# A hybrid conv/attention encoder step: one more projection block by seven products, two plain gates fewer, gate outputs in pairs of pieces, and another form and order of the loads between attention and the output products

## The chip, the cores and the metric

One core of a Trainium2 chip runs the whole program. The metric is device microseconds of one execution. The kernel before takes 1477.87 us (median of 3 runs, 1476.27 to 1478.02). All times are from those runs, from one profiled execution, or from its trace.

## What is computed

One inference step of a one-layer encoder: 1024 new prompt frames and 64 frames of a running stream, 1024 channels each, all in fp32. Cut to what matters:

```python
def mixer(xn, conv_prefix, attn_fn, w_in, w_conv, w_conv_out, w_attn_out, w_out):
    proj = xn @ w_in                                  # 1024 -> 5120
    cb, cc, ch, q, k, v, ga, gb = jnp.split(proj, ...)
    cv, conv_state = causal_conv(cc * ch, conv_prefix, w_conv)
    ya = (cb * cv) @ w_conv_out                       # 512 -> 1024
    o, new_k, new_v = attn_fn(heads(q), heads(k), heads(v))
    yb = o.reshape(B, L, ATT_DIM) @ w_attn_out        # 512 -> 1024
    merged = jax.nn.sigmoid(ga) * ya + jax.nn.sigmoid(gb) * yb
    return merged @ w_out, conv_state, new_k, new_v
# trunk: x += mixer(rmsnorm(x)); x += swiglu(rmsnorm(x)); rmsnorm(x)
# outputs too: the last 512 key and value rows; for the running stream its
# cache, rolled by 64 rows (448 old rows are copied, 64 new ones appended)
```

The gate projections `ga` and `gb` are 1024 channels wide: eight blocks of 128 rows each, over all T = 1088 frames.

## The kernel before

**Numbers.** Every fp32 operand is split into a high part (rounded to fp32r, the format the matmul takes) and a low part, what is left. A product is three matmuls: weights high by data high, weights high by data low, weights low by data high. `split(hi, lo, src)` does it with a copy on ACT and a subtraction on DVE (L126 to L130).

**Two ways to multiply.** A `Unit` (L202, `run` L246) computes two blocks of 128 output channels for all frames by a seven-product scheme of 2x2 blocks: 7 products x 4 slices of the contraction x 3 matmuls x 2 pieces of 272 frames = 168 matmuls of 128x272. Its inner loop gives each weight to two pieces `j` in turn, into two banks of one PSUM tile. A plain block goes through `product` (L323): for one piece of 272 frames, 24 matmuls in a row where the contraction is 1024 long, 12 where it is 512. Two plain blocks of 1024 take 2 x 4 pieces x 24 = 192 matmuls.

**Stages.** (1) normalisation, transposes, V. (2) twelve units: q, k, cc, ch, cb and two of the four pairs of blocks of `gb` (blocks 0 to 3), with the convolution on the side. The convolution's result times `cb` is u; `cb_done` (L699) splits it and stores both parts to DRAM in `u_d`. (3) the twelve plain gates of `GATES` (L335): eight blocks `a` and blocks 4 to 7 of `b`. `gate` (L805) copies each piece of 272 frames from PSUM (tag `mm`, 3 banks) to a buffer `gst` of `st_pool` (5 buffers) on ACT and stores it to DRAM through the POOL queue. Attention runs in between: `between()` (L1003) is called after a piece and lets `PER` = 2.7 of attention's 75 steps be emitted. (4) with `LAST` = 3 gates to go, what is left of attention is emitted, its buffers are given up, and u, the attention output ob, its reciprocal sums rc, and the first gates ga and gb are loaded on SP's queue (L1049 to L1066). ob times rc is split on chip. (5) the output products ya (from u) and yb (from ob), for m = 0 to 7, four pieces each, multiplied by the sigmoid of the gates out of PSUM (L1075 to L1100). (6) `w_out`, the second norm, twenty-two units of the up projections, the down projection, the final norm. In the ups, two copies from DRAM to DRAM (L1539) fill the old rows of the two cache outputs.

**Order.** The kernel is written in Tile: the program says which buffers and operations there are, and a scheduler that works before the run sets the order on each engine. Engines and queues then issue strictly in that order and wait on semaphores. In the names, `g` is a gate's PSUM bank (`g_2` is the piece that starts at frame 544), `gst` its buffer in SBUF, `wp` a plain weight (high), `low` the area of low parts, `xn` the normalised input, `pv`, `t`, `s` attention's PSUM tiles, `rc` the reciprocal sums.

The layouts matter to the change: `Acts` (L56) finds a slice of u or ob at `[:, l, k, o]` with rows of 1088 frames; the operands of the units keep two halves of 544 frames with padding between the parts (`operand`, L136).

```python
def product(out, w, x, o, n):
    kt = 4 * len(w)
    for k in range(kt):
        ...
        mm(out, a, first, start=k == 0, stop=False)
        mm(out, a, then, start=False, stop=False)
        mm(out, b, p, start=False, stop=k == kt - 1)
```

## Time and profile before

| What | Value |
|---|---|
| profiled execution | 1475.81 us |
| its span (first to last instruction) | 1473.8 us |
| median of the runs | 1477.87 us |
| PE busy | 1458.0 us, 10200 matmuls |
| DVE / ACT / POOL busy | 979.2 / 678.1 / 133.1 us |
| DMA | 264.72 MB, mean 180 GB/s |
| twelve units and what is between them | 68.3 to 323.1 us |
| gates with attention | 323.1 to 575.0 us |
| output products ya, yb | 575.0 to 671.1 us |

The page lists the busy time of each engine and the groups of instructions. Matmuls are pipelined: a record of a 272-column matmul is about 0.29 us long, but the next starts 0.12 to 0.13 us after it, so the pace has to be read from the starts of matmuls, not from their lengths, and a wait shorter than some 0.16 us leaves no idle time in the PE row.

### The profile page before, as it was taken

To read this page: it belongs to the slowest core of one execution; us is meant where nothing else is said; L and a number is where in the kernel's file an instruction comes from. 1 tells how busy PE (TensorE), PEld (TensorE's weight loads), DVE (VectorE), ACT (ScalarE), POOL (GpSimd) and SP (SyncE) were. 2 spreads that over 40 slices of the span, in tenths; PEclk is the share of its full clock that TensorE was granted. 3 is DMA by queue.
4 is the path that set the end of the run, shared out by engine and by line. 5 is a ranking of instruction groups with operands and counts; after the bars stand their busy time and mean duration, and the time that the engine had idled before them with its cause. 6 is when DMAs were issued, how large, how long until landed. Compare 5 with 4: busy or idle time off the path is not lost.

```text
span 1473.8 us, 26481 instructions
## 1 busy us (share of the span) xinstructions
PE 1458.0 (99%) x10200; PEld 1369.7 (93%) x10200; DVE 979.2 (66%) x1850; ACT 678.1 (46%) x1396; POOL 133.1 (9%) x243
## 2 busy tenths in 40 slices
PE   8999999999999999999999999999999999999997
PEld 6899999999999999998889999999999999888886
DVE  7975465633776753763489767666666768957676
ACT  7644333434776753631355444444444445412223
POOL 1400010001111121000100111110011111000000
PEclk9999999999999999999999999999999999999999
DMA  8586523178766539544433454433344448777675
GB/s 292 177 271 224 177 93 113 60 212 233 190 191 176 152 101 326 186 126 136 147 114 108 147 183 162 161 140 120 119 149 159 149 161 308 256 233 248 212 268 203
DMA packets 164029, 264.72 MB, mean 180 GB/s; under 512 B 18624, under 2 KB 98688, under 8 KB 163872
## 3 DMA queue, kind: packets, MB, share of 16 engines
q1 hardware_dynamic: 143040, 196.13, 42.4%
q0 software_dynamic: 19712, 64.81, 12.2%
q10 hardware_dynamic: 1152, 2.10, 0.4%
q8 instruction: 80, 1.31, 0.4%
q14 instruction: 45, 0.37, 0.1%
HBM read 172.89 MB, written 91.92 MB: 180 GB/s over the span
## 4 chain that ended last, share of the span: by engine, by line
PE 92%; DVE 3%; DMA 2%; ACT 1%; SPq 1%; issue 1%; ACTq 0%; DVEq 0%
PE Ab L266 9%; PE Aa L266 8%; PE A L1637 8%; PE Db L266 4%; PE Da L266 4%; PE D L1637 4%; PE g L330 2%; PE g L331 2%; PE g L332 2%; PE B L1637 2%; PE Bb L266 2%; PE Ba L266 2%; PE wo L1139 2%; PE wo L1141 2%; PE wo L1140 2%; PE t L952 2%
## 5 line engine op out<-in xcount | busy, mean ns | idle before, releaser
L330 PE MATMUL g<-xn,wp 128*128 128x272 f32 x384 | 112.7, 293 | 0.0
L331 PE MATMUL g<-xn,wp 128*128 128x272 f32 x384 | 111.6, 291 | 0.0
L332 PE MATMUL g<-xn,low 128*128 128x272 f32 x384 | 110.6, 288 | 0.0
L128 ACT CAST ring<-w2r 128x512 fp32r<-128x512 f32 (+1 forms) x78 | 42.6, 587 | 89.0 <-PE A L1637 50.8
L128 ACT CAST hq<-sa 128x512 fp32r<-128x512 f32 x73 | 45.2, 620 | 81.0 <-DVE sa L1335 55.2
L863 DVE CUSTOM_DVE_ANT_0 p<-s,bb 128x640 f32<-128x640 f32 (+5 forms) x72 | 47.5, 661 | 42.5 <-DMA qd<-q_d 26.2
L1319 POOL DMA_DIRECT2D h_d<-hq x73 | 38.9, 533 | 400.4 <-DVE hq L129 230.7
L330 PEld LDWEIGHTS g<-xn,wp 128*128 128x128 f32 x384 | 72.3, 188 | 1.0
L332 PEld LDWEIGHTS g<-xn,low 128*128 128x128 f32 x384 | 72.3, 188 | 0.5
L331 PEld LDWEIGHTS g<-xn,wp 128*128 128x128 f32 x384 | 72.3, 188 | 0.1
L1637 PE MATMUL A<-ring,low 128*128 128x512 f32 x264 | 72.3, 389 | 0.0
L1637 PE MATMUL A<-ring,ht 128*128 128x512 f32 x264 | 72.2, 389 | 0.0
L129 DVE TENSOR_TENSOR hq<-sa,hq 128x512 fp32r<-128x512 f32 x73 | 50.3, 689 | 28.0 <-ACT hq L128 27.8
L129 DVE TENSOR_TENSOR low<-rawa,wa 128x512 fp32r<-128x512 f32 x55 | 37.7, 686 | 40.2 <-ACT wa L128 40.2
L1637 PEld LDWEIGHTS A<-ring,low 128*128 128x128 f32 x264 | 49.6, 188 | 10.3
L266 PE MATMUL Aa<-tt,wa 128*128 128x272 f32 x352 | 57.8, 285 | 1.3 <-ACT sa_Q L254 1.3
L1637 PEld LDWEIGHTS A<-ring,ht 128*128 128x128 f32 x264 | 49.5, 188 | 10.3
L266 PE MATMUL Aa<-mg,wa 128*128 128x272 f32 x352 | 57.8, 286 | 0.5 <-DVE sa L1300 0.5
L266 PE MATMUL Ab<-mg,wb 128*128 128x272 f32 x352 | 58.0, 286 | 0.0
L266 PE MATMUL Ab<-tt,wb 128*128 128x272 f32 x352 | 57.8, 285 | 0.0
L129 DVE TENSOR_TENSOR ring<-w2r,ring 128x512 fp32r<-128x512 f32 (+1 forms) x78 | 48.6, 645 | 11.1 <-ACT ring L128 10.9
L128 ACT CAST wa<-rawa 128x512 fp32r<-128x512 f32 x55 | 34.0, 620 | 47.0 <-PE Ab L266 33.3
(543 smaller groups left out, 4485.5 us busy)
## 6 DMA issues: line engine op xcount, KB each, us to landing
h_d<-hq POOLq DMA_DIRECT2D x73, 512.0 KB, 3.4
ht<-h_d SPq DMA_DIRECT2D x77, 256.0 KB, 3.6
low<-h_d SPq DMA_DIRECT2D x77, 256.0 KB, 3.6
rawa<-in_w_ff SPq DMA_DIRECT2D x11, 1024.0 KB, 5.7
rawb<-in_w_ff SPq DMA_DIRECT2D x11, 1024.0 KB, 5.3
w2r<-in_w_ff SPq DMA_DIRECT2D x11, 1024.0 KB, 7.0
qd<-q_d SPq DMA_DIRECT2D x32, 272.0 KB, 4.4
rawp<-in_w_in SPq DMA_DIRECT2D x6, 1024.0 KB, 6.3
```

The source lines that it names most:

```text
L128: a = act.copy(hi, src)
L129: b = vec.tensor_tensor(lo, src, hi.bitcast(F32), op=ALU.subtract)
L266: newest[0] = mm(t[:, j, :HN], w[:, k, :], x[p][:, k, l, j * HN : (j + 1) * HN], start=p in (1, 2, 7) and k == 0 and n == 0, stop=k == 3 a ...
L330: mm(out, a, first, start=k == 0, stop=False)
L331: mm(out, a, then, start=False, stop=False)
L332: mm(out, b, p, start=False, stop=k == kt - 1)
L863: vec.tensor_tensor_reduce(out=s if len(ps.shape) == 2 else s.rearrange("p (a b) -> p a b", a=2), in0=ps, in1=bias if len(ps.shape) == 2 e ...
L952: nc.tensor.transpose(tp[:, i * P : (i + 1) * P], s[:, i * P : (i + 1) * P], ident)
L1139: mm(ps, x(k, 0), wh, start=f, stop=False)
L1140: mm(ps, x(k, 1), wh, start=False, stop=False)
L1319: stored[0] = nc.gpsimd.dma_start(h_d[p, c - 1], hq.rearrange("p i l t -> p (i l t)").bitcast(F32)).ins
L1637: mm(t, ht[k][:, j, x], w[:, l], start=p in (1, 2, 7) and k == 0 and n == 0, stop=k == len(ks) - 1 and n == 2, skip_group_check=p in (6, 5 ...
```

## The change

- `PER` 2.7 becomes 3.15, `LAST` 3 becomes 2.
- A unit ("gb", 2) is added between ("ch", 1) and ("cb", 1): thirteen units. `GATES` loses blocks 4 and 5 of `b`: ten plain gates.
- `product2` computes two pieces at once: for each slice and each of the three products, the same weight goes to two pieces, into two banks. It serves the gates when two pieces are asked for (the first four gates' first halves, and all of the last two gates), and all of ya and yb, whose PSUM tiles now have two banks (2 tiles for 5 of one bank). What reads them (sigmoid, multiply, add, split) works on 544 frames at a time instead of 272.
- u is stored as one fp32 row instead of two parts, loaded first of all into the place of its low part, and split on chip. u and ob get a layout with halves of 544 frames, 32 elements of padding and 40 elements between the parts.
- `st_pool` has 3 buffers for 5. Weights of ya and yb have their low part at the same place as others (no `at` of 40), and a step of the counter of the low slots is dropped before `w_out`.
- The gates `ga` are loaded in halves of 544 frames instead of quarters.
- The 448 old rows of each cache are copied in eight DMAs of 56 rows, one in each of sixteen ups, instead of one DMA for each.

```diff
-PER = 2.7
-LAST = 3
+PER = 3.15
+LAST = 2
...
     def at(self, l, k, o, n):
-        return self.t[:, l, k, o : o + n]
+        h = o // HT
+        a = h * (HT + 32) + o - h * HT
+        return self.t[:, l, k, a : a + n]
...
+    def product2(outs, w, x, o):
+
+        kt = 4 * len(w)
+        for k in range(kt):
+            a, b = (t[:, k % 4] for t in w[k // 4])
+            for n, (s, l) in enumerate(((a, 0), (a, 1), (b, 0))):
+                for j in range(2):
+                    mm(
+                        outs[j], s, x.at(l, k, o + j * HN, HN),
+                        start=k == 0 and n == 0, stop=k == kt - 1 and n == 2,
+                    )
+
-    GATES = [("a", m) for m in range(8)] + [("b", m) for m in range(4, 8)]
+    GATES = [("a", m) for m in range(8)] + [("b", m) for m in range(6, 8)]
...
-        ("cb", 1), ("gb", 1),
+        ("gb", 2), ("cb", 1), ("gb", 1),
...
-            st = stage()
-            split(st[:, 0], st[:, 1], s)
-            nc.sync.dma_start(u_d[2 * u + r, :, :, h * HT : (h + 1) * HT], st.bitcast(F32))
+            nc.sync.dma_start(u_d[2 * u + r, :, h * HT : (h + 1) * HT], s)
...
-    st_pool = pg_stack.enter_context(tc.tile_pool(name="st_pool", bufs=5, reuse_waits="tile"))
+    st_pool = pg_stack.enter_context(tc.tile_pool(name="st_pool", bufs=3, reuse_waits="tile"))
...
-        for c in cs:
+        pss = [pmm.tile([P, 512], F32, tag="mm", name=f"g{i}_{c}") for c in cs]
+        if len(cs) == 2:
+            product2([ps[:, :HN] for ps in pss], gate_w[i], xn, PIECES[cs[0]][0])
+        else:
+            product(pss[0][:, :HN], gate_w[i], xn, *PIECES[cs[0]])
+        for c, ps in zip(cs, pss):
...
+            for q in range(4):
+                nc.sync.dma_start(u.rows(1, q).bitcast(F32), u_d[q].rearrange("p (h t) -> p h t", h=2))
+                split(u.rows(0, q), u.rows(1, q), u.rows(1, q).bitcast(F32))
             for k in range(4):
-                if k == 3:
+                if k == 2:
                     gates_in("ga", 0)
-                for q in {0: (0,), 1: (1,), 2: (), 3: (2, 3)}[k]:
-                    nc.sync.dma_start(u.t[:, :, q].bitcast(F32), u_d[q])
...
-        for c in range(4):
-            gate(i, (c,))
-            between()
+        if i < len(GATES) - LAST:
+            for c in range(4):
+                gate(i, (c,))
+                between()
+        else:
+            gate(i, (0, 1))
+            gate(i, (2, 3))
...
-    psum2 = pg_stack.enter_context(tc.tile_pool(name="psum2", bufs=5, space=PSUM, reuse_waits="tile"))
+    psum2 = pg_stack.enter_context(tc.tile_pool(name="psum2", bufs=2, space=PSUM, reuse_waits="tile"))
...
-                ya = psum2.tile([P, 512], F32, tag="mm", name=f"ya{m}_{o}")
-                product(ya[:, :n], wa, u, o, n)
-                vec.tensor_tensor(t, ya[:, :n], t, op=ALU.mult)
+                ya = psum2.tile([P, 2, 512], F32, tag="mm", name=f"ya{m}_{o}")
+                product2([ya[:, j, :HN] for j in range(2)], wa, u, o)
+                t = t.rearrange("p (j n) -> p j n", j=2)
+                vec.tensor_tensor(t, ya[:, :, :HN], t, op=ALU.mult)
...
-        taken[0] += 1
...
-        if n in (4, 6):
-            nm, src = (("k", ck), ("v", cvv))[n // 2 - 2]
+        if 2 <= n < 18:
+            nm, src = (("k", ck), ("v", cvv))[(n - 2) // 8]
+            a = (n - 2) % 8 * 56
             with tc.issue_after(stored[0]):
-                nc.gpsimd.dma_start(outs[f"cache_{nm}_sample"][: CACHE - TS], src[TS:])
+                nc.gpsimd.dma_start(outs[f"cache_{nm}_sample"][a : a + 56], src[TS + a : TS + a + 56])
```

**How the order moves.** On PE, where the last but one gate goes from one piece or pair to the next. Before, the third piece ends and the fourth begins in another bank (the three banks go round):

```order
L330 MATMUL g_2_6566<-xn_100,wp_4_6074 128x272
L331 MATMUL g_2_6566<-xn_100,wp_4_6074 128x272
L332 MATMUL g_2_6566<-xn_100,low 128x272
L330 MATMUL g_3_6594<-xn_99,wp_0_6071 128x272
L331 MATMUL g_3_6594<-xn_99,wp_0_6071 128x272
L332 MATMUL g_3_6594<-xn_99,low 128x272
```

Now the pair of pieces 0 and 1 ends and the pair of 2 and 3 begins:

```order
L346 MATMUL g_0_6583<-xn_98,low 128x272
L346 MATMUL g_1_6584<-xn_98,low 128x272
L346 MATMUL g_2_6639<-xn_99,wp_0_6100 128x272 x2
L346 MATMUL g_2_6639<-xn_99,low 128x272
L346 MATMUL g_3_6640<-xn_99,wp_0_6100 128x272 x2
L346 MATMUL g_3_6640<-xn_99,low 128x272
L346 MATMUL g_2_6639<-xn_99,wp_0_6100 128x272
L346 MATMUL g_3_6640<-xn_99,wp_0_6100 128x272
```

With three banks in turn, `g_3_6640` takes the bank that `g_0_6583` had, two matmuls before the pair's change; three matmuls to `g_2` stand ahead of it.

On ACT, the same stretch, before (`gst` are copies out of the gates' banks, `rc` to `ob` the split of the attention output):

```order
L813 COPY gst_3_6619<-g_3_6594 128x272
L813 COPY gst_0_6653<-g_0_6628 128x272
L128 CAST ob<-rc_6462 128x1088
L813 COPY gst_1_6681<-g_1_6656 128x272
L813 COPY gst_2_6709<-g_2_6684 128x272
L813 COPY gst_3_6737<-g_3_6712 128x272
L128 CAST ob<-rc_6470 128x1088
```

and with the change:

```order
L831 COPY gst_0_6633<-g_0_6583 128x272
L831 COPY gst_1_6636<-g_1_6584 128x272
L133 CAST wp_0_7005<-rawp_7003 128x512
L133 CAST u<-u 128x2x544 x2
L831 COPY gst_2_6689<-g_2_6639 128x272
L831 COPY gst_3_6692<-g_3_6640 128x272
L133 CAST wp_0_7074<-rawp_7003 128x512
L133 CAST u<-u 128x2x544 x2
L831 COPY gst_0_6750<-g_0_6700 128x272
L831 COPY gst_1_6753<-g_1_6701 128x272
```

The casts of u, which wait for u's loads, now stand ahead of the copies that free the banks of the last but one gate's second pair.

On SP's queue, the loads after attention's last stores (`o_d<-co_s`), before:

```order
L888 DMA o_d<-co_s 64x32 x2
L1053 DMA u<-u_d 128x2x1088
L1055 DMA ob<-o_d 128x1088
L1059 DMA rc_6462<-rc_d 64x1088 x2
L1053 DMA u<-u_d 128x2x1088
L1055 DMA ob<-o_d 128x1088
L1059 DMA rc_6470<-rc_d 64x1088 x2
L1055 DMA ob<-o_d 128x1088
L1059 DMA rc_6477<-rc_d 64x1088 x2
```

and with the change:

```order
L906 DMA o_d<-co_s 64x32 x2
L1072 DMA u<-u_d 128x2x544 x4
L1078 DMA ob<-o_d 128x2x544
L1082 DMA rc_6546<-rc_d 64x1088 x2
L1078 DMA ob<-o_d 128x2x544
L1082 DMA rc_6553<-rc_d 64x1088 x2
L1040 DMA ga_0_6559<-ga_d 128x544
L1040 DMA ga_544_6561<-ga_d 128x544
L1078 DMA ob<-o_d 128x2x544
L1082 DMA rc_6564<-rc_d 64x1088 x2
L1078 DMA ob<-o_d 128x2x544
L1082 DMA rc_6571<-rc_d 64x1088 x2
```

All of u, half as many bytes, now comes ahead of ob and rc; before, two of its four blocks came after the first three of ob.

More of the change, by code (lines that the diff above doesn't have):

```diff
@@ L62, in at, with rows @@
     def at(self, l, k, o, n):
[L63 removed]
+        h = o // HT
+        a = h * (HT + 32) + o - h * HT
+        return self.t[:, l, k, a : a + n]
+    def rows(self, l, k):
+        return self.t[:, l, k].rearrange("p (h t) -> p h t", h=2)[:, :, :HT]
 @with_exitstack
@@ L94, in encoder_kernel @@
     x21_d = dr.tile([P, 2, 4, HT], F32, name="x21_d")
-    u_d = dr.tile([4, P, 2, T], F32, name="u_d")
+    u_d = dr.tile([4, P, T], F32, name="u_d")
     q_d = dr.tile([NH, HD, 2, T], F32, name="q_d")
@@ L1061, in encoder_kernel @@
                     )
+                r = r.rearrange("p (h t) -> p h t", h=2)
                 vec.tensor_tensor(r, o, r, op=ALU.mult)
-                split(ob.t[:, 0, k], ob.t[:, 1, k], r)
+                split(ob.rows(0, k), ob.rows(1, k), r)
             with tc.issue_after(ld.ins):
```

45 lines of the change are left out of this document (23 added, 22 removed).

## The prediction

> **What bounds the kernel now.** First the page: part 1 and the group of chains.
>
> ```profile
> PE 1458.0 (99%) x10200; PEld 1369.7 (93%) x10200; DVE 979.2 (66%) x1850; ACT 678.1 (46%) x1396; POOL 133.1 (9%) x243
> PE 92%; DVE 3%; DMA 2%; ACT 1%; SPq 1%; issue 1%; ACTq 0%; DVEq 0%
> ```
>
> PE is busy for 1458.0 of 1473.8 us, and the chain that ended last is PE for 92%. The list of who waited for whom, for PE alone, shows how little there is to win by taking waits away:
>
> ```profile
> PE warm L443 <- ACT ones L441: 2.9, 1, 2.9
> PE Aa L266 <- ACT sa_Q L254: 1.3, 1, 1.3
> ...
> PE s L905 <- DVE mx L863: 0.5, 2, 0.3
> PE t L952 <- DVE pt L129: 0.2, 1, 0.2
> ```
>
> No wait on a load, none in the output products. So the change pays through the number of matmuls and their pace, and costs through new waits. The stages, by the windows from the last two units to the end of the output products:
>
> ```profile
> core 0: us, PE busy (x) PEld busy (x) DVE busy (x) ACT busy (x) POOL busy (x), PEclk, DMA share, GB/s
> 302.41:323.13 20.72, 20.72 (x171) 20.72 (x169) 8.71 (x14) 7.32 (x14) 0.63 (x5) 1.00 0.68 219
> 323.13:347.09 23.96, 23.96 (x195) 23.96 (x194) 0.69 (x1) 3.78 (x9) 3.81 (x7) 1.00 0.91 271
> 347.09:542.06 194.97, 193.74 (x1395) 178.88 (x1393) 137.23 (x327) 136.36 (x320) 32.29 (x62) 1.00 0.60 164
> 542.06:575.04 32.98, 32.98 (x265) 32.98 (x265) 10.33 (x11) 10.94 (x21) 5.90 (x11) 1.00 0.93 313
> 575.04:671.07 96.03, 96.03 (x771) 96.03 (x769) 64.47 (x159) 45.79 (x126) 0.54 (x1) 1.00 0.53 164
> ```
>
> The granted clock is 1.00 throughout. One unit (168 matmuls; the counts take in neighbours at the edges) lasts 20.72 us, 123.3 ns each. The first eight gate pieces (192) last 23.96 us, 124.8 ns each. The output products (16 blocks of 48, 768) last 96.03 us, 125.0 ns each. The edges of these windows are starts of matmuls:
>
> ```profile
> 302.41 0.66 PE L266 MATMUL Agb<-xn,wgb 128*128 128x272 f32 x4
> ...
> 323.13 0.29 PE L330 MATMUL g<-xn,wp 128*128 128x272 f32 x1
> ...
> 575.04 0.29 PE L330 MATMUL ya<-u,wp 128*128 128x272 f32 x1
> ...
> 671.07 0.40 PE L1143 MATMUL wo<-low,ms 128*128 128x512 f32 x1
> ```
>
> **The change part by part.**
>
> *Two gates go, a unit comes.* Removed: 192 matmuls at 124.8 ns, 23.96 us. Added: one unit, 20.72 us. PE has no idle time in either stretch, so both count whole: -3.2 us. The unit's own work on DVE and ACT (8.71 and 7.32 us in the window of a gb unit) hides under its 20.72 us.
>
> *Pace in pairs.* `product2` issues in the order of the units, with the distances of their layout. If it runs at their 123.3 ns, ya and yb win 96.03 - 768 x 0.1233 = 1.3 us, and the gates in pairs (four half gates of 48, two gates of 96: 384) 384 x 1.5 ns = 0.6 us. Together -1.9 us; bounds 0 (the pace stays) and -1.9, since the unit's pace is the best 272-column row. I take all of it: same shapes, same clock, same order.
>
> [...]
>
> *The step between pairs.* Three banks go round, so a pair's second bank is the first of the pair before (the order on PE shows three matmuls put ahead of it). How soon is it free? A copy out of a gate's bank and the last matmul before it:
>
> ```profile
> 548.29 0.39 ACT L813 COPY gst<-g 128x272 f32<-128x272 f32 x1 [2.61 <-PE g L332]
> ...
> 547.97 0.29 PE L332 MATMUL g<-xn,low 128*128 128x272 f32 x1
> ```
>
> From start to start 0.32 us, and the copy takes 0.39: the bank is free 0.71 us after its last matmul began. PE has five others to issue meanwhile (one of the pair, three of the next, its own pace), 0.62 us. That leaves 0.1 us, with the wake-up (not in the trace, no more than a matmul's 0.12) up to 0.2. There are five such steps (three in the first gates, two in the last; before the last gate nine matmuls go ahead): +0.5 us, bounds 0 and 1.0. That `gst` has three buffers for five costs nothing by itself: a store is needed back after two copies more, some 6 us, and where it comes late the copy waits, not yet PE.
>
> *Attention in 24 pieces for 28.* The stretch 347.09:542.06 loses 4 pieces, 4 x 3.0 = 12.0 us of matmuls that fill waits, so DVE's share goes from 137.23 / 194.97 (70%) to 137.23 / 183 (75%), ACT's from 70% to 75%. Neither becomes the bound. The idle time there is 194.97 - 193.74 = 1.2 us; waits too short to show lie on top. A typical one: the last gate matmul starts at 364.10, the transposes after it at 364.31, 0.21 us instead of 0.125.
>
> ```profile
> 364.10 0.29 PE L330 MATMUL g<-xn,wp 128*128 128x272 f32 x1
> 364.31 0.77 PE L952 MATMUL t<-ident,p 128*128 128x128 f32 x5
> ```
>
> Such an 0.08 us in none or in half of the 75 steps more is 0 to 3.0 us. I take 0.5: each wait still has 7.7 gate matmuls per step to cover it, where it had 9.
>
> *The loads between attention and the products.* They are the tight place. Before, on SP, DVE and ACT:
>
> ```profile
> 544.25 0.59 SPq L1053 DMA_DIRECT2D u<-u_d  x1
> ...
> 555.04 1.29 DVE L1062 TENSOR_TENSOR rc<-ob,rc 128x1088 f32<-128x1088 f32 x1 [2.52 <-DMA rc<-rc_d]
> 563.26 1.29 DVE L1062 TENSOR_TENSOR rc<-ob,rc 128x1088 f32<-128x1088 f32 x1 [4.43 <-DMA rc<-rc_d]
> 568.00 1.29 DVE L1062 TENSOR_TENSOR rc<-ob,rc 128x1088 f32<-128x1088 f32 x1 [0.98 <-DMA rc<-rc_d]
> 584.69 1.28 DVE L129 TENSOR_TENSOR ob<-rc,ob 128x1088 fp32r<-128x1088 f32 x1
> ...
> 581.79 0.80 ACT L1082 ACTIVATE ga<-ga 128x272 f32<-128x272 f32 x2 [6.12 <-DMA ga<-ga_d]
> ...
> L814 POOL DMA_DIRECT2D gb_d<-gst x13: 539/539/578, 537.0 to 576.3; - x13
> ```
>
> DVE's multiplications that waited for rc tell when each block was there. ob and rc of a block alone (third row less second): 4.7 us. With a block of u ahead (second less first): 8.2, so u's block takes 3.5. The first took 544.25 to 555.04, 10.8, so 2.6 is start-up. The rest, up to the ga at 581.79, which is queued right behind the last rc, is 13.8 = ga 1.9 + 2 x 3.5 + 4.7 and some. Now with u in half the bytes and ahead: 2.6 + 4 x 1.75 + 4 x 4.7 + 1.9 = 30.3 us, less the stores of the gate that is gone on the same engines (4 of the 13 in the last row, about 1 us): the last rc lands 29.3 us after the first load's issue, 573.5 on the old scale. When is it needed? Attention's last product is at 541.15:
>
> ```profile
> 541.15 0.91 PE L964 MATMUL pv<-pts,vsd 128*128 128x128 f32 x5
> ...
> 579.83 0.44 DVE L1085 TENSOR_TENSOR ga<-ya,ga 128x272 f32<-128x272 f32 x1 [0.31 <-PE ya L332]
> ...
> 556.41 1.10 ACT L128 CAST ob<-rc 128x1088 fp32r<-128x1088 f32 x1 [1.69 <-DVE rc L1062]
> ```
>
> Behind it PE now has 168 gate matmuls from about 541.6 (20.7 us, and 0.5 for steps between pairs) and 96 of ya (11.8): yb begins at 574.6, where it began at 587.1. On DVE the last rc's multiplication (1.29 us) stands ahead of the one that frees the PSUM tile that yb takes (544 columns, two of the 0.44 us rows of 272): yb waits until 573.5 + 2.2 = 575.7. That is +1.1 us; I take 1.0. Bounds: 0, if ob and rc move faster without u between them; and if a half block of u takes as long as an ob, which now has its shape (4.7 less rc's part, about 3.0), u costs 12.0 instead of 7.0 and the wait is 6 us. The split of u on chip (4 x 1.10 us on ACT, 4 x 1.29 on DVE, by the ob rows of that size) lies in a stretch where ACT and DVE are busy 10.9 and 10.3 of 32.98 us. But the casts stand ahead of the copies that free a bank on ACT (the order shows it): the second block of u has to be cast by 551.8, and is there by 544.25 + 2.6 + 3.5 = 550.4, cast by 551.5. No cost, no margin.
>
> *Nothing from the rest.* The cache copies move the same bytes, and PE had no wait in the ups after their first unit, at either copy: 0, and 16 issues of 0.5 us on a POOL that is 9% busy.
>
> ```profile
> L1539 POOL DMA_DIRECT2D out_cache_k_sample<-in_cache_k x1: 516/516/516, 870.3 to 870.3; - x1
> ```
>
> The instructions on 544 columns save DVE and ACT overhead in a stage where they are 67% and 48% busy: 0. The moved low slots could change the pace of `w_out`'s 416 matmuls; no row prices it, 0.
>
> *Sum:* -3.2 - 1.9 + 0.5 + 0.5 + 1.0 = -3.1 us on the profiled execution's 1475.81 (span 1473.8 and 2.0 around it): 1472.7. The median of the runs lies 2.06 us above that execution, so I forecast 1477.87 - 3.1 = **1474.8 us**, 0.21% faster.
>
> **Rivals.**
>
> *The pace does not change*: the 125 ns come from the 272 columns and the load of a weight for each, not from order and places. Then -3.2 + 2.0 = -1.2: 1476.7. For it: gates and outputs have different layouts and nearly one pace (124.8 and 125.0). Against it: the unit, with as many columns and as many weight loads, is at 123.3. [...]
>
> *The operands come late*, on the other side. Place: yb's first matmul, and before it ACT's queue, where u's casts hold the copies of the second pair. Price: every microsecond that the last rc lands after 572.4. With u at ob's price it lands at 578.5, yb waits 6.1: -3.2 - 1.9 + 1.0 + 6.1 = +2.0, 1479.9; with the start-up twice as long, 1482.5. It eats the gain if the last rc lands after about 576.5, and slows the kernel by more than 0.2% after 579.5. For it: a DMA share of 0.93 in the stretch, and u's loads now shaped like ob's. Against it: they carry half the bytes and begin at once.
>
> *Attention is too dense*: 3.0 instead of 0.5 us and one exposed softmax (0.83 us on ACT, the row below, and as much on DVE) per head, 8 x 0.8 us: -3.1 + 2.5 + 6.4 = +5.8, 1483.7. Against it: both engines at 75%.
>
> ```profile
> 523.83 0.83 ACT L873 ACTIVATE p<-p,mx 128x640 f32<-128x640 f32 x1
> ```
>
>
> *All hides*: no wait at all, -5.1: 1472.8.
>
> **How the numbers follow.** A difference under 0.2% (3 us) is about what a measurement of this kernel cannot tell from none. Forecast (1473.4 to 1476.4) 0.45, of which 0.28 lie beyond 0.2%; all hides 0.16, faster; pace unchanged 0.10, within; late operands 0.21, of which 0.16 slower and 0.05 within; dense attention 0.08, slower. So faster 0.44, same 0.32, slower 0.24. The range leaves out a tenth on each side: below, all hidden and the fastest run's 1.6 us, 1471.2; above, the middle of the late operands, 1481.0.
>
> **What would show it.** Thirteen units of 20.72 us; ya and yb in 94.7 us of matmuls plus waits; the first four half gates in 23.7 us plus 0.1 at each step between pairs. In PE's waits: rows of g on ACT's gst (steps between pairs; long ones mean u's casts), rows of yb on DVE's ga (the last rc). In the loads: the four blocks of u landed within some 10 us of the first issue. The forecast is wrong if the pace of ya stays at 125.0, if yb waits over 3 us, or if the stretch with attention loses less than 10 us.

## The result, and the profile after

The changed kernel takes 1482.72 us (median of 16 runs, 1478.37 to 1489.99) where the kernel before takes 1477.4 in the runs beside it: ratio 1.0035 [1.0023, 1.0047]. It is slower by a third of a per cent; 1474.8 was forecast. The profiled execution took 1486.28 us, its span is 1484.2. It is the second slowest of the 16, 3.6 us above their median, so its profile shows more loss (10.4 us of span) than the medians do (5.3 us).

The page (busy time; chain of waits), then PE's list of who waited for whom, of the changed kernel:

```profile
PE 1460.8 (98%) x10176; PEld 1369.8 (92%) x10176; DVE 979.7 (66%) x1792; ACT 674.3 (45%) x1343; POOL 136.1 (9%) x249
PE 73%; issue 18%; DMA 3%; DVE 2%; ACT 2%; POOL 1%; SPq 0%; POOLq 0%; ACTq 0%; DVEq 0%
```

```profile
PE Aa L271 <- ACT sa_Q L259: 5.2, 4, 1.6
PE yb L346 <- DVE ga L1114: 4.0, 1, 4.0
...
PE wo L1172 <- DVE ms L134: 0.4, 1, 0.4
```

yb's row is new: it waits 4.0 us for DVE. So is the small one of wo. The 1.3 us that `Aa` waited for ACT before have become 5.2 in four waits. There is no row of g on gst for PE's matmuls. The windows by stage (from the first gate to the first ya, to the first wo, to the first up, to the downs; columns as in the windows before):

```profile
343.12:572.92 229.80, 228.12 (x1658) 211.89 (x1657) 146.29 (x338) 146.03 (x338) 37.11 (x70) 1.00 0.68 189
572.92:676.09 103.17, 99.14 (x770) 98.92 (x769) 62.17 (x97) 45.17 (x84) 1.08 (x2) 0.97 0.53 162
676.09:778.44 102.35, 101.96 (x474) 83.17 (x473) 53.17 (x111) 36.68 (x72) 9.26 (x17) 1.00 0.44 143
778.44:1249.80 471.36, 465.14 (x3738) 462.71 (x3736) 333.46 (x563) 217.67 (x413) 54.14 (x102) 1.00 0.43 151
```

Before the change, the last two of these stages were:

```profile
671.07:772.74 101.67, 101.67 (x474) 83.34 (x473) 53.00 (x111) 37.23 (x74) 9.25 (x17) 1.00 0.44 144
772.74:1239.30 466.56, 464.21 (x3738) 462.42 (x3737) 333.15 (x562) 217.60 (x413) 46.88 (x88) 1.00 0.43 152
```

Beside the same edges in the trace of before, in us:

| stage | before | after | change | forecast |
|---|---|---|---|---|
| up to the first gate (one unit more) | 323.1 | 343.1 | +20.0 | +20.7 |
| gates and attention | 251.9 | 229.8 | -22.1 | -23.6 |
| ya, yb | 96.0 | 103.2 | +7.1 | -0.3 |
| w_out | 101.7 | 102.4 | +0.7 | 0 |
| ups | 466.6 | 471.4 | +4.8 | 0 |
| the rest | 234.5 | 234.4 | -0.2 | 0 |
| span | 1473.8 | 1484.2 | +10.4 | -3.1 |

So the unit and the gates did about what was forecast. The time went in two places.

**ya and yb.** PE, DVE and ACT of the changed kernel around the wait (timeline: start, length, what; in brackets the idle time before and what ended it):

```profile
584.51 0.41 PE L346 MATMUL ya<-u,low 128*128 128x272 f32 x2
588.96 1.27 PE L346 MATMUL yb<-ob,wp 128*128 128x272 f32 x4 [4.03 <-DVE ga L1114]
```

```profile
581.82 1.29 DVE L1086 TENSOR_TENSOR rc<-ob,rc 128x1088 f32<-128x1088 f32 x1 [1.59 <-DMA rc<-rc_d]
584.28 1.29 DVE L134 TENSOR_TENSOR ob<-rc,ob 128x1088 fp32r<-128x1088 f32 x1 [1.17 <-ACT ob L133]
586.33 1.29 DVE L1086 TENSOR_TENSOR rc<-ob,rc 128x1088 f32<-128x1088 f32 x1 [0.75 <-DMA rc<-rc_d]
588.18 0.72 DVE L1114 TENSOR_TENSOR ga<-ya,ga 128x544 f32<-128x544 f32 x1 [0.56 <-ACT ga L1110]
```

```profile
587.49 0.66 ACT L1110 ACTIVATE ga<-ga 128x544 f32<-128x544 f32 x1 [3.24 <-DMA ga<-ga_d]
```

Read it backwards. yb's first matmul needs the PSUM tile that the multiplication at 588.18 gives back. That one stands on DVE behind the multiplication with the last rc, which arrived at 586.3, and needs the sigmoid of a ga that is loaded behind that rc and arrived at 587.5. And the wait costs more than its length, as two windows inside yb and the one across the wait show:

```profile
584.90:588.96 4.06, 0.03 (x2) 0.01 (x1) 2.69 (x3) 1.47 (x2) 0.00 (x0) 0.90 0.99 349
588.10:594.90 6.80, 5.95 (x26) 5.95 (x27) 2.70 (x4) 4.54 (x8) 0.00 (x0) 0.50 0.79 273
600.00:676.00 76.00, 76.00 (x608) 76.00 (x607) 45.98 (x78) 31.21 (x62) 0.00 (x0) 1.00 0.42 134
```

The granted clock falls to 0.50 until 594.9: 26 matmuls in 5.95 us, 2.7 us more than at 123.3 ns. After it the clock is 1.00 again, but the pace is not 123.3 ns: from the first start in the last window to the last (606 matmuls, 75.96 us; the 608 take in neighbours) it is 125.6 ns, and up to the first wo that is another 1.5 us. From start to start yb comes 4.2 us late. So 4.2 + 2.7 + 1.5 = 8.4 of the 8.5 us that the stage lies above 768 x 123.3 ns.

This is the price in one execution. In two other profiles of the same kernel (again and third, below) yb came 2.7 and 2.6 us late, the pace stayed at 123.3 ns, and only third had a low clock; the stage took 97.4 and 98.7 us, 2.7 and 4.0 above 94.7 (again, then third):

```profile
573.18:670.61 97.43, 95.00 (x770) 94.79 (x769) 61.39 (x97) 45.43 (x84) 1.08 (x2) 1.00 0.54 171
```

```profile
573.18:671.89 98.71, 96.44 (x770) 96.22 (x769) 61.51 (x97) 45.29 (x84) 1.08 (x2) 0.98 0.52 168
```

**The ups.** Three units wait where none did. POOL, ACT and PE of the changed kernel around the longest:

```profile
914.28 0.53 POOL L1347 DMA_DIRECT2D h_d<-hq  x1 [0.78 <-DVE hq L134]
915.49 0.53 POOL L1347 DMA_DIRECT2D h_d<-hq  x1 [0.67 <-DVE hq L134]
920.45 0.53 POOL L1347 DMA_DIRECT2D h_d<-hq  x1 [4.43 <-DVE hq L134]
```

```profile
918.81 0.62 ACT L133 CAST hq<-sa 128x512 fp32r<-128x512 f32 x1 [4.00 <-DMA h_d<-hq]
...
922.48 0.60 ACT L259 COPY sa_Q<-Aa 128x544 f32<-128x544 f32 x1
```

```profile
923.13 0.77 PE L271 MATMUL Aa<-tt,wa 128*128 128x272 f32 x4 [1.63 <-ACT sa_Q L259]
```

ACT stands 4.00 us because no buffer of `hq` is free: a store of h, the one issued at 910.93, has not landed. The copy of `Aa` that PE needs is queued behind. The list of DMA traffic from 917 to 921.5 us, in 40 slices, shows what holds the stores up:

```profile
DMA  9979979998920000000000000000000000000000
GB/s 446 437 328 400 510 291 437 510 437 328 400 73 0 36 36 36 0 36 36 0 36 36 36 0 36 36 0 36 36 36 0 36 36 36 0 36 0 0 0 0
```

The traffic stops at 918.3 and then trickles for 2.7 us at some 25 GB/s, about a sixteenth of the 437 before. The trace marks the landing of a transfer in sixteen parts, and here the last part is late. Of the store that ACT waits for, fifteen parts had landed by 915.80, the last at 918.71. The stores issued at 914.28 and 915.49 had fifteen parts landed by 917.36 and 918.75 and the last at 920.25 and 921.47: that is the trickle. A weight load that SP issued at 908.64 was as late in its last part (914.54 and 917.47).

That one of the sixteen DMA engines was late is my reading of these numbers; no row names an engine, or says why. The late part does not hang on GpSimd issuing the store: in two of the runs below (four_sp, before_sp) SP issues the stores of h, and there the last part came over 0.6 us behind the fifteenth in 43 of 117 stores, where it did in 251 of 784 stores issued by GpSimd (stores in the ups whose sixteen marks are in the traces).

### The profile page after: what moved, and what is told of

Read it like the earlier page. It is cut to its first block, busy times and chain, and to the rows that moved or that the text cites. A ratio compares the mean times of both kernels' runs of the same rounds, so it can differ in the third digit from the quotient of the medians.

```text
span 1484.2 us, 26292 instructions
## 1 busy us (share of the span) xinstructions
PE 1460.8 (98%) x10176; PEld 1369.8 (92%) x10176; DVE 979.7 (66%) x1792; ACT 674.3 (45%) x1343; POOL 136.1 (9%) x249
## 4 chain that ended last, share of the span: by engine, by line
PE 73%; issue 18%; DMA 3%; DVE 2%; ACT 2%; POOL 1%; SPq 0%; POOLq 0%; ACTq 0%; DVEq 0%
PE A L1666 8%; PE Ab L271 7%; PE Aa L271 7%; PE D L1666 4%; PE Db L271 4%; PE Da L271 3%; PE Agb L271 2%; PE B L1666 2%; PE Bb L271 2%; PE g L346 2%; PE t L970 2%; PE Ak L271 2%; PE Aq L271 2%; PE Acc L271 2%; PE Acb L271 2%
## 5 line engine op out<-in xcount | busy, mean ns | idle before, releaser
L335 PE MATMUL g<-xn,wp 128*128 128x272 f32 x192 | 57.2, 298 | 0.0
L337 PE MATMUL g<-xn,low 128*128 128x272 f32 x192 | 56.4, 294 | 0.0
L891 ACT ACTIVATE p<-p,mx 128x640 f32<-128x640 f32 (+5 forms) x72 | 50.9, 707 | 11.6 <-DVE mx L881 10.0
L336 PE MATMUL g<-xn,wp 128*128 128x272 f32 x192 | 55.8, 290 | 0.0
L134 DVE TENSOR_TENSOR ring<-w2r,ring 128x512 fp32r<-128x512 f32 (+1 forms) x78 | 48.8, 646 | 10.5 <-ACT ring L133 10.4
L271 PEld LDWEIGHTS Aa<-tt,wa 128*128 128x128 f32 x352 | 49.2, 189 | 6.0 <-ACT sa_Q L259 6.0
L1168 PE MATMUL wo<-low,mg 128*128 128x512 f32 x128 | 50.9, 397 | 0.0
```

Of the source, the lines that this page charges most:

```text
L134: b = vec.tensor_tensor(lo, src, hi.bitcast(F32), op=ALU.subtract)
L271: newest[0] = mm(t[:, j, :HN], w[:, k, :], x[p][:, k, l, j * HN : (j + 1) * HN], start=p in (1, 2, 7) and k == 0 and n == 0, stop=k == 3 a ...
L891: act.activation(s, s, AF.Exp, bias=mx, scale=-1.0, accum_out=sm)
L1168: mm(ps, x(k, 0), wh, start=f, stop=False)
```

## The experiments

Ratios are to the kernel before on the same chip; "gap" is the time from the start of one matmul to the next.

### Does yb wait for the last rc, and is it worth 4 us?

*last_three*: three gates behind attention.

```diff
-PER = 3.15
-LAST = 2
+PER = 3.78
+LAST = 3
```

> The changed kernel with three gates behind attention instead of two, and 20 pieces in it, 3.78 steps to each. Theory (the wait of yb and the low clock behind it come from an rc that lands 4 us too late): the loads begin some 10 us earlier against the products, the last rc lands before it is needed, no row of yb waiting for DVE's ga, the granted clock 1.00 after it, minus 7 to 8 us in ya and yb; ya, yb and their waits last 95 us. Attention in 20 pieces costs 0 to 4 us of it: 1475 to 1479. Rival (dense attention): the stretch from the first gate to the first ya gets 6 us longer or more and eats the gain, 1481 to 1484. Rival (the low clock is not from the wait): a stretch at 0.5 stays, with no wait before it.

*no_rc*: three of the four loads of rc are left out, so three blocks of ob are not divided by their sums.

```diff
-                for j in range(2):
+                for j in range(2 if k == 0 else 0):
...
-                vec.tensor_tensor(r, o, r, op=ALU.mult)
+                vec.tensor_tensor(r, o, r if k == 0 else o, op=ALU.mult)
```

> The changed kernel with three of the four loads of rc left out (the second to the fourth block of o is multiplied by itself instead, so the DVE's work is the same and those rows are not divided by their sums). Theory (the bytes of rc are what makes the last block late, 4.7 us for ob and rc together, about 1.7 of it rc): the last ob lands 5 us earlier, yb waits 0 and the clock stays at 1.00: the median 1475 to 1476. Rival (the transfers are bound by the start of each or by u's shape): the last ob lands at most 2 us earlier, a wait of 2 us or more for DVE's ga remains.

*best1*: last_three, the casts of u behind the copies of the second gate, the cache rows in two copies as before the change.

```diff
+            gate_w[i + 1] = next_w()
+            for e in (i, i + 1):
+                gate(e, (0, 1))
+                gate(e, (2, 3))
+            with tc.issue_after(copied[i + 1, 3]):
+                for q in range(4):
+                    split(u.rows(0, q), u.rows(1, q), u.rows(1, q).bitcast(F32))
```

> Three gates behind attention with 20 pieces in it (as the run with three gates), the casts of u behind the copies of the second of these gates, and the cache rows in two copies. Theory (the two gates fewer and the pace are worth 3 us and more; what ate them are the wait of yb with its low clock and the sixteen copies): the row of g waiting 2.1 us for ACT's gst and the low clock after it go, no wait of yb, no wait for sa_Q beyond the one of 1.3 us: span 1467 to 1470, 4 to 7 us under the kernel before; the median at 1471 to 1474. Rival (the ends move: later casts make ya late, or a denser attention shows): a row of ya on DVE's or ACT's u of 2 us or more, 1475 or above.

*last_four*: best1 with `PER = 4.72`, `LAST = 4`; *four_two* is the same kernel again.

> As the run best1 (casts of u behind the copies of the second gate after attention, cache rows in two copies), but with four gates behind attention and 16 pieces in it, 4.72 steps to each. Theory (yb waits because the last rc lands some 32 us after the first issue of u, and the issue starts only when attention's last stores are away): the issue starts some 4 us earlier against the first ya, the last rc lands before yb needs it, no waits of ya or yb and no low clock: ya and yb in 94.7 us, the two stages from the first gate to wo 3 to 5 us shorter than in best1. Rival (attention in 16 pieces is too dense): the stretch of gates grows by 3 us or more and takes it back.

> The version with four gates behind attention and the cache rows in two copies, again. Its profiled span was 1472.1 us, 1.7 under that of the kernel before, its median equal to it. No wait of yb and ya and yb in 94.8 us again; the median from 1474 to 1478: with chance waits in the ups as in the kernel before, 2 to 3 us under it; with more of them, equal to it.

| kernel | median | ratio | gates | ya, yb |
|---|---|---|---|---|
| last_three | 1478.54 | 1.0009 [0.9998, 1.0021] | 232.7 | 94.7 |
| no_rc | 1483.21 (5 runs) | 1.0043 [1.0029, 1.0058] | 229.8 | 96.5 |
| best1 | 1479.25 | 1.0010 [0.9997, 1.0022] | 229.1 | 100.0 |
| last_four | 1477.24 | 1.0000 [0.9986, 1.0014] | 230.8 | 94.8 |
| four_two | 1478.29 | 1.0008 [0.9997, 1.0020] | 232.3 | 95.2 |

Where the loads come in time, the wait, the low clock and the slow pace go together: 94.7 and 94.8 us, what 768 matmuls take at 123.3 ns. Window of ya and yb, and the loads and the last rc of last_four:

```profile
573.95:668.78 94.83, 94.83 (x770) 94.78 (x769) 59.79 (x97) 42.08 (x81) 1.08 (x2) 1.00 0.51 164
```

```profile
547.71 3.04 SPq L1074 DMA_DIRECT2D u<-u_d  x4
```

```profile
581.46 1.29 DVE L1094 TENSOR_TENSOR rc<-ob,rc 128x1088 f32<-128x1088 f32 x1 [0.66 <-DMA rc<-rc_d]
```

```profile
585.79 0.66 PE L346 MATMUL yb<-ob,wp 128*128 128x272 f32 x4
```

From the first issue of u to the last rc it still takes 33.8 us; but the loads now start 38.1 us ahead of yb, where in the changed kernel they start 31.0 us ahead of the time at which yb would have begun without its wait. In no_rc the last ob landed at 576.3, some 8 us before that of the changed kernel where 5 were expected, though only two of the three loads of rc that it leaves out stand ahead of that ob; yb did not wait, though ya did for 1.5 us. Its median did not fall: in its profile the ups took 474.7 us, 3.4 more than in the changed kernel's, with the slow pace that the last section shows. So this run shows that the loads make yb wait, and not what the wait is worth in the median.

last_three was half a miss and best1 a miss (1471 to 1474 was expected), and they show how tight the place is. In last_three the row of g waiting for ACT that the prediction's second rival spoke of appeared, because a cast of u stood ahead of the copy of a gate's bank, and with it the low clock (PE's timeline, then a window):

```profile
562.49 0.82 PE L346 MATMUL g<-xn,wp 128*128 128x272 f32 x2 [2.05 <-ACT gst L831]
```

```profile
562.50:565.90 3.40, 3.40 (x15) 3.40 (x16) 2.88 (x3) 1.75 (x3) 1.07 (x2) 0.50 1.05 257
```

best1 took this wait away; its gates were 3.5 us shorter, so yb came sooner against the same loads and waited 2.1 us for them again, and ya 1.0. With four gates both waits were gone. Attention in 16 pieces cost little: 230.8 us for the gates in last_four and 232.3 in four_two, where the changed kernel has 229.8.

### Do the sixteen copies make the stores of h late?

*two_copies* and, on another chip, *two_again*: the changed kernel with the two copies of before. *sixteen_alone*: the kernel before with the sixteen. *sp16*: the changed kernel, copies issued by SP; but they are ordered behind a store on another queue, POOL's, and as in four_sp below they did not stay behind it: they ran at the start, from 21.6 to 48.0 us, and none in the ups. *third* is the changed kernel again; *four_sixteen* is last_four with the sixteen.

```diff
-        if 2 <= n < 18:
-            nm, src = (("k", ck), ("v", cvv))[(n - 2) // 8]
-            a = (n - 2) % 8 * 56
+        if n in (4, 6):
+            nm, src = (("k", ck), ("v", cvv))[n // 2 - 2]
```

> The changed kernel with the cache rows copied by two transfers, in the fifth and the seventh unit of the ups, as before. Theory (the sixteen copies make the stores of h late, and so the three waits of 1.3 to 1.9 us for ACT's sa_Q in the ups): the three waits go, the ups last 461 us for the 466 of the changed kernel, the median falls by 4 to 5 us to about 1478. Rival (the copies have no part in it; the waits come from the new places in PSUM and SBUF or from the weight loads, which moved in time with the whole kernel): the waits stay, 1482 to 1483. The wait of yb stays under both.

> The kernel before with only the cache rows' copies in sixteen. Theory (the copies make the stores of h late): rows of Aa waiting for ACT's sa_Q in the ups, 3 to 5 us in all, the median at 1481 to 1482. Rival (no part in it): no such row beyond the one of 1.3 us, the median at 1477 to 1478.

> The changed kernel with the sixteen cache copies issued by SP instead of POOL. Theory one (what hurts is a copy in POOL's queue, between the stores of h): no wait for sa_Q beyond the one of 1.3 us, the ups at 467 to 468 us, the median at 1479. Theory two (what hurts is the traffic of the copies, spread over sixteen units instead of two): the waits stay, 1482 to 1483. A third way: the weight loads in SP's queue come later behind the copies and PE waits for wa or wb, over 1483.

> The changed kernel as it is, on the same chip as the next three. Median 1481.5 to 1483 by the runs so far. With the next run: if the sixteen copies cost, 2 to 4 us above it; if the waits in the ups are chance alone, within 1.5 us of it.

> The changed kernel with the cache rows in two copies, as in the first call. Theory (sixteen copies cost): median 1478 to 1480, 2 to 4 us under the run before it. Rival (chance): 1481 or above, within 1.5 us of the run before it.

> The same with the cache rows in sixteen copies. Theory (sixteen copies cost): median 2 to 4 us above the run before it, more rows of Aa waiting for ACT's sa_Q. Rival (chance): within 1.5 us of it.

| sixteen copies | median, ratio | two copies | median, ratio |
|---|---|---|---|
| sixteen_alone | 1479.46, 1.0015 [1.0004, 1.0026] | (before) | 1477.28, 1 |
| sp16 | 1482.01, 1.0025 [1.0010, 1.0040] | two_copies | 1479.05, 1.0006 [0.9996, 1.0017] |
| third | 1481.86, 1.0028 [1.0017, 1.0038] | two_again | 1482.07, 1.0027 [1.0015, 1.0038] |
| four_sixteen | 1478.10, 1.0014 [1.0002, 1.0025] | four_two | 1478.29, 1.0008 [0.9997, 1.0020] |

The first two rows spoke for a cost of 2 to 4 us, and I believed it. The second is no evidence: it compares two chips, the same kernel (two_copies, two_again) came out at 1.0006 and at 1.0027 on two chips, and sp16 has no copy in the ups at all:

```profile
L1568 SPq DMA_DIRECT2D out_cache_k_sample<-in_cache_k x8: 510/587/596, 21.6 to 40.3; - x8
L1568 SPq DMA_DIRECT2D out_cache_v_sample<-in_cache_v x8: 587/683/1594, 40.9 to 48.0; - x8
```

The other three rows are pairs on one chip, and they differ. With the change in the kernel (the last two rows) the copies cost nothing: -0.2 us between the medians in both, 0.01 and 0.06% between the ratios. In the kernel before (the first row) they cost 2.2 us between the medians, and the interval of the ratio, 0.04 to 0.26%, does not reach zero. So no cost is shown for the changed kernel, as priced; 0.1% either way would not be seen, and the first row stays unexplained.

### If not the copies, what?

*before_shift* and *after_shift*: both kernels with 104 tiny instructions that nobody waits for. *again* and *before_look* (one run): second profiles of both.

```diff
+    for n in range(40):
+        nc.gpsimd.memset(some_p, 0.0)
+        if n < 32:
+            vec.memset(some_v, 0.0)
+            act.copy(some_a, cols[:, 13:14].to_broadcast([P, 2]))
```

> The kernel before with 40 more tiny memsets on POOL, 32 on DVE and 32 tiny copies on ACT at the start of attention, each on a tile that nobody reads; all else stands in the same order. They move the places in the ups at which these engines' next instructions are fetched (the instruction queues in the list of DMA queues) against the stores of h. Theory one (the waits for sa_Q come where such a fetch, or another chance event, meets the stores of h; which units it hits is a matter of the count of instructions ahead, and an edit that adds some moves them): waits of 1 us or more in one to three units of the ups, the median 1 to 3 us over that of the kernel before. Theory two (the waits come from what the change does in the ups, the sixteen copies): no wait beyond the one of 1.3 us, and a median within 0.6 us of the kernel before.

> The changed kernel with the same tiny instructions at the same place. Theory one (chance meetings set by the count of instructions): the waits in the ups sit in other units than in both profiles of the changed kernel, and the median may move to either side by 1 to 3 us of 1482. Theory two (the sixteen copies): one to three waits again, 1481.5 to 1483. The wait of yb stays at 2 to 4 us under both.

> The changed kernel as it is, for a second profile and more times beside the kernels of this call. Theory (the sixteen copies make stores of h late, so that waits for ACT's sa_Q come in some of the ups): one to three such waits of 1 to 2 us, in the ups up to the one with the last copy or soon behind it, perhaps at other units than in the first profile; the wait of yb of 4 us as before; median 1482 to 1483. Rival (the three waits were an accident of one execution): none beyond the one of 1.3 us, and a median near the 1479.05 of the run with two copies.

> The kernel before, for a second profile. If its ups are clean by their build, no wait for sa_Q beyond the one of 1.3 us in this execution too; if they are clean by chance, one or more of 1 to 2 us.

Medians: before_shift 1479.63, ratio 1.0005 [0.9994, 1.0017]; after_shift 1484.29, 1.0039 [1.0024, 1.0054]; again 1481.93, 1.0032 [1.0020, 1.0044]. The kernel before has such waits too, here in before_look:

```profile
956.57 0.77 PE L266 MATMUL Aa<-tt,wa 128*128 128x272 f32 x4 [1.24 <-ACT sa_Q L254]
```

And the changed kernel has them where no copy is left; in after_shift the last copy is issued at 1130.1 (POOL), and PE waits at 1172.65 and 1215.41:

```profile
1130.11 0.50 POOL L1574 DMA_DIRECT2D out_cache_v_sample<-in_cache_v  x1
```

```profile
1172.65 0.76 PE L271 MATMUL Aa<-tt,wa 128*128 128x272 f32 x4 [1.25 <-ACT sa_Q L259]
1215.41 0.77 PE L271 MATMUL Aa<-tt,wa 128*128 128x272 f32 x4 [1.04 <-ACT sa_Q L259]
```

I counted gaps over 0.9 us at this place in twenty profiles, ten places in each (every second unit). In the ten kernels with sixteen copies: 12 in the 63 places whose stores of h go out between the first copy and the last, 7 in the 37 whose stores go out before or after (all ten of sp16 among them, with one gap). The rate is the same, 0.19 in both. With two copies: 9 in 100. So the waits come without the traffic of the copies; that the kernels with sixteen had twice as many has no explanation here.

In part they follow the program. Of the ten places, the changed kernel has them at the first, third and fourth in its first profile, at the first and fourth in again, at the first, third and fourth in third. With the tiny instructions ahead they sit at the fourth, sixth, ninth and tenth; in the kernel before at none and at the fourth, with the tiny instructions at the second and fourth. But of the other two kernels that were profiled twice, each has none in one profile and one in the other (two_again the first place, four_two the seventh). This fits theory one, that which stores have a late part depends on the instructions that went before, and that an edit deals the places anew; with two shifted profiles it is not shown. The changed kernel was dealt two or three of them. What makes the last part late is open. The traces have one hint, and it is the fetch of instructions that theory one named: of 294 stores of h whose last part came over 0.6 us behind the fifteenth, 191 have a packet of one of the queues that carry instructions between 1 us before their issue and 3 us after it, of the 607 others 113. No run tests whether that is the cause, nor is it shown that the tiny instructions moved these packets. The medians are too wide to show the price by themselves: before_shift lies 2.4 us above the kernel before on its chip, with a ratio of 1.0005, and after_shift has no changed kernel beside it.

*four_sp* and *before_sp*: the stores of h issued by SP.

```diff
-            stored[0] = nc.gpsimd.dma_start(h_d[p, c - 1], ...
+            stored[0] = nc.sync.dma_start(h_d[p, c - 1], ...
```

> The version with four gates behind attention and two copies, with the stores of h issued by SP. Theory (ACT waits for a buffer of hq because a store on POOL's queue lands 6 to 8 us after its issue where 3 to 4 are usual): issued by SP they start sooner and land in time, no wait for sa_Q beyond the one of 1.3 us, the ups at 467 us, the median at 1474 to 1475, 2 to 3 us under the kernel before. Rival (the engines of the DMA are late, whoever issues, or the stores now stand behind the weight loads in one queue): waits as before or more, 1477 or above.

> The kernel before with the stores of h issued by SP. Theory: its chance waits go too, the median falls by 1 to 1.5 us to its fastest runs, 1475 to 1476. Rival: the same median or a higher one.

Both came out 12 to 13 us slower (1491.47 and 1489.81; 1.0100 [1.0074, 1.0126] and 1.0086 [1.0069, 1.0103]), for a reason of my edit: the two cache copies were ordered behind a store on POOL's queue, that store was gone from it, and they ran at the start, ahead of the first inputs (POOL of before_sp):

```profile
1.33 0.64 POOL L1539 DMA_DIRECT2D out_cache_k_sample<-in_cache_k  x1 [0.38 <-issue]
...
2.30 0.55 POOL L1539 DMA_DIRECT2D out_cache_v_sample<-in_cache_v  x1
```

All behind the start is 12 to 14 us late. The ups took 467.3 and 467.5 us in their profiles, without a wait for sa_Q over 0.7 us but the usual one. That is too little to say that the stores are better placed on SP.

### Where does the pace come from?

*no_pairs*: the same layout, the two pieces of a pair one after the other.

```diff
-        for k in range(kt):
-            a, b = (t[:, k % 4] for t in w[k // 4])
-            for n, (s, l) in enumerate(((a, 0), (a, 1), (b, 0))):
-                for j in range(2):
+        for j in range(2):
+            for k in range(kt):
+                a, b = (t[:, k % 4] for t in w[k // 4])
+                for n, (s, l) in enumerate(((a, 0), (a, 1), (b, 0))):
```

> The changed kernel with the same layout and distances, but the two pieces of a pair one after the other instead of by turns. If the pace of 123.3 ns comes from the turns (two matmuls with one weight block, one bank after the other), ya and yb go back to 125.0 ns, 96.0 us beside their waits; if it comes from the set distances of the layout, they stay at 123.3 ns, 94.7 us. The wait of yb may shift by up to 1 us.

Median 1482.73 (8 runs), 1.0033 [1.0017, 1.0049]. Windows over the first four half gates and from the first to the 96th matmul of ya; the changed kernel, then no_pairs:

```profile
343.12:367.64 24.52, 24.50 (x194) 23.89 (x193) 0.69 (x1) 3.26 (x8) 3.25 (x6) 1.00 0.94 274
572.92:584.64 11.72, 11.72 (x98) 11.72 (x96) 6.29 (x7) 5.84 (x8) 1.08 (x2) 1.00 1.06 278
```

```profile
343.07:367.10 24.03, 24.03 (x195) 24.03 (x193) 0.69 (x1) 3.84 (x9) 3.81 (x7) 1.00 0.93 272
572.06:583.91 11.85, 11.85 (x98) 11.85 (x96) 7.79 (x9) 6.55 (x9) 0.89 (x2) 1.00 1.05 290
```

95 gaps of ya in 11.72 us are 123.4 ns, in 11.85 us 124.7: most of the gain over 125.0 is the turns, the rest the layout. The pace is that of the program and not of one execution: every profile with turns has 123.3 ns here, but for no_rc and best1, where a wait of ya falls into the stretch. In the gates it goes the other way: 24.52 with turns, 24.03 without. There the weight load waits for the copy that frees the bank, at each of the five changes of pair, and PE's starts at a change come 0.26 to 0.31 and 0.23 us apart where 0.12 is usual; no_pairs has no such start at a change. Who waited for `gst`, in the changed kernel:

```profile
  PEld g L346: 1.1, 5
```

## Why the prediction was wrong, step by step

- **Two gates go, a unit comes (-3.2).** Right: +20.0 up to the first gate (0.7 less than the unit, because the start before the first gb unit was 0.7 us shorter), and the removed gates show in the next stage.
- **Pace in pairs (-1.9).** Right for ya and yb: 94.7 us in last_three, 1.3 under before. The rival that the pace does not change is refuted by no_pairs: same columns, same loads of weights, 1.4 ns apart.
- **The step between pairs (+0.5).** Mis-sized, with the 0.6 that pairs were to win in the gates. The first four half gates, forecast at 23.7 and three steps of 0.1, 24.0, took 24.52; the whole stretch of gates and attention is 0.8 us shorter without turns (229.0 in no_pairs). Five steps cost some 1.3 us by PE's starts, where 0.5 was forecast: the bank that comes free late costs more than the turns bring. The wake-up, which the prediction put at no more than 0.12, can be read in the ups: PE starts at 923.13, 0.05 us after the copy on ACT that it waits for ends (922.48 and 0.60).
- **Attention in 24 pieces (+0.5).** The stretch from the 193rd gate matmul to the first one behind attention's last product (347.08 to 541.99 before, 367.64 to 551.45 now) lost 11.1 of the 12.0 us, about 0.9 for the 0.5. Rival three, dense attention, is refuted by this and by last_four's 16 pieces.
- **The loads (+1.0).** This is the step that failed. u did as priced: the first rc multiplication at 568.0 is 14.3 us behind the first issue of u (553.75), and 2.6 + 7.0 + 4.7 is 14.3. From there to the last rc the sum had 3 x 4.7 + 1.9 - 1.0 = 15.0 us, the trace has 586.33 - 568.0 = 18.3. The blocks took 6.5, 7.3 and 4.5 us, where the sum had 4.7, 6.6 and 4.7 and took 1.0 off for four stores of the gate that is gone (eight stores still run beside the loads, where eleven did): the two blocks around ga 0 cost more. Why is open; in the second to fourth block the last of the sixteen parts of ob landed 1.3 to 1.9 us behind the fifteenth, where it was 0.5 to 0.8 before. Then a ga queued behind the last rc, which I had not followed, added 0.6. So yb waited 4.2 us from start to start, and 2.7 and 2.6 in again and third. That is the forecast's own sign of being wrong in the first profile (over 3 us), and not in the other two. And the prediction priced a wait at its length. Behind 4.03 us of idle PE the clock was 0.50 for 6.8 us and the pace slow for the rest: 8.5 us in place of 1.0 in this execution, 2.7 and 4.0 in the other two. Rival two named this place, a late last rc, and gave 6.1 us of wait, +2.0 in all, and a chance of 0.21; but its reason, u at ob's price, did not come true, and it had no term for the clock. last_three and last_four, on which yb does not wait and the stage takes 94.7 and 94.8 us, are the proof.
- **Nothing from the rest (0).** The cache copies: no cost in two pairs on one chip, 2.2 us in a third with the kernel before. w_out: +0.7, with a wait for `ms`, since the last split is on 544 frames. The ups: the profile of before had no wait behind the first unit, and I read that one execution as a property of the kernel. Its second profile has one wait more; the changed kernel's three have two or three, 3 to 6 us in the stage.

The forecast missed the difference of the medians by 8.4 us: -3.1 forecast, +5.3 measured. The loads are 2 to 4 of these by the two pairs on one chip, with the wait of yb and without it: third against four_sixteen and two_again against four_two are 3.8 us apart in the medians, 0.14 and 0.19% (2 to 3 us) in the ratios. These versions differ in the gates and the casts of u too. The rest is the ups (3 to 6 us in the profiles), the steps between pairs, attention and w_out, by single profiles and so only argued. last_four, four_two and four_sixteen, without yb's wait, stand at 1477.24 to 1478.29, the changed kernel at 1481.86 to 1482.72. What is left against the kernel before is between -0.14% and +0.25% by the three intervals. last_four's profile, without such waits in the ups, has a span of 1472.1, 1.7 us under that of before; no median showed this gain, and no version tried beats the kernel before.

## What to carry to other kernels

When an edit removes matmuls ahead of a point where loads are due, it moves the due time forward and leaves the loads where they are: add up the whole queue of loads from its first issue, block by block, with what is queued behind the last one too, and price a wait on PE as long as those that had a low clock behind them here (1.84 to 4.49 us) at its length plus what that clock may take afterwards (in last_three, behind 2.05 us, 15 matmuls in 3.40 us, some 1.6 us more than at 123.3 ns). Do not read "no wait" in one execution as a property; profile twice. Compare versions that differ by 0.2% on one chip, in one set of runs.

## What the hardware showed that I had not expected

The low clock came behind each of yb's six waits of 3.8 to 4.5 us: 0.50 for 6.8 us in the changed kernel (4.03) and in after_shift (3.89), for 3.4 us in two_copies, two_again, sp16 and no_pairs (3.82 to 4.49). Around 2 us the length did not tell. Behind 1.84 us (four_sp), 1.99 (sixteen_alone), 2.05 (last_three), 2.06 (best1) and 2.27 (third, yb) it was 0.50 for 3.4 us. Behind 1.97 us (third, in the ups), 2.05 (after_shift, in the ups) and 2.43 (again, yb) it stayed at 1.00, as it did behind the 1.63 in the ups of the changed kernel. The window behind yb's wait in again:

```profile
587.60:591.00 3.40, 3.39 (x27) 3.40 (x28) 1.98 (x3) 3.27 (x6) 0.00 (x0) 1.00 0.72 208
```

In these eleven cases the low clock lasted 3.4 us nine times and 6.8 us, twice that, two times; waits of 1.84 to 2.27 us were enough for it five times. No run tells what decided it around 2 us.

The same 168 matmuls ran at two paces with the same granted clock. In sp16 every unit takes 20.72 us up to a wait at 919.7, and 21.09 from there to the last; windows of one unit ahead of it and one behind:

```profile
885.38:906.10 20.72, 20.72 (x171) 20.72 (x169) 12.64 (x21) 7.93 (x16) 1.06 (x2) 1.00 0.25 87
1139.82:1160.91 21.09, 21.09 (x170) 21.09 (x169) 12.70 (x21) 8.22 (x16) 1.06 (x2) 1.00 0.26 91
```

The same happened in the profiles of no_rc (from 956 us on), before_shift (1083) and third (1169), always from a wait on, and to yb in the changed kernel (125.6 for 123.3 ns, where 21.09 us for 168 are 125.5), there in the first profile alone: behind the waits of yb in again, third, after_shift, two_copies, two_again and sp16 the pace is 123.3. No run tells why.
